# A hybrid decoder layer on one core: inverse sums turned by the matmul engine, attention outputs kept in two parts, scratch and tables moved

## The chip, the core and the metric

The kernel runs on one core of one Trainium2 chip. Its time is the device time in microseconds (us). Before the change it is 1889.12 us, the median of 3 runs (1889.0 to 1889.23). A core has five engines that run side by side, each through its own instructions in a fixed order: PE (matmul), DVE and POOL (elementwise work), ACT (activations and copies) and SP, which here only starts transfers (DMAs). ACT starts some DMAs too. An instruction that waits holds up everything behind it on its engine.

## The reference

One layer works on 16 learned meta tokens and 1024 real tokens of width 1024. Three mixers run side by side on the normalised input, their outputs go through one projection, and a gated feed-forward follows:

```python
hn = rmsnorm(h, mix_norm_g[i])
proj = hn @ w_in[i]
sb_q, sb_k, sb_v, ssm_z, ssm_xbc, ssm_dt, c_q, c_kv, k_r = jnp.split(proj, split_at, axis=-1)
o_sb  = stick_breaking_attention(sb_q, sb_k, sb_v, valid)      # 8 heads of 64
o_ssm = ssd_mixer(ssm_z, ssm_xbc, ssm_dt, ...)                 # 16 heads, chunks of 128
o_mla = mla_attention(q_mla, k_mla, v_mla, valid)              # 8 heads, rotary part of 32
h = h + jnp.concatenate([o_sb, o_ssm, o_mla], axis=-1) @ w_out[i]
fn = rmsnorm(h, ffn_norm_g[i])
h = h + (jax.nn.silu(fn @ w_gate[i]) * (fn @ w_up[i])) @ w_down[i]
return rmsnorm(h, final_norm_g)[:, BLOCK:, :]
```

The softmax of `mla_attention` divides each query's row by its sum. `ssd_mixer` needs running sums of the decay, `dt * a`, inside each chunk of 128 tokens.

## The kernel before

**Precision.** Every large product is made of three matmuls: each operand is split into an upper part, rounded to the matmul type, and a lower part, what is left. The upper part is a copy on ACT and the lower one a subtraction on POOL or DVE. `dense_fm` (L129 to L142) runs such a product over column chunks, with `dpool`'s two PSUM banks (`d_ps`) for the sums and an `evac` function that takes each sum away.

**Order of work.** The program lists its work stage by stage. When it is built, a planner gives each engine a fixed order: it goes by a simulated time, takes the earliest listed instruction that is ready, and fills gaps with later stages. Tiles of one tag share a number of slots; a new tile gets a slot once the last reader of the tile that held it is done.

The stages that matter here, by lines:

- *First projections* (from L607). `raws` (L214) are four weight buffers taken from the slots that later hold the keys of the stick-breaking heads: `raws[2]` and `raws[3]` from tag `K`, which has four slots. Pair 0 of the heads takes the two other `K` slots (`sb_project`, L575); pair 1 takes those of `raws[2]` and `raws[3]`. `k_evac` (L588) writes them.
- *`step_sizes`* (L411). After the step sizes come the decay sums `AT`; three blocks of them are turned on PE into banks of the pool `tp` (two banks, `acst`), copied by ACT to `acs`, and split by DVE into three bf16 parts in `A3` (L463 to L470). `acs` is a tile of tag `cacc`, two slots. `A3` is read first in the chunk scan (L765).
- *Stick-breaking attention* (`sb_attend`, L677). For each of 8 heads and 4 pairs of query blocks, `weighted_values` (L293) turns the weights on PE (banks `ptm`, `ptg` of `tp`), splits them, multiplies them with the values and adds two halves into `oT` (64 x 256, L343), which ACT stores to `s_osb` (L349). Projections of the next pair and the convolution units fill PE in between.
- *Chunk scan and latents* (L727 to L911). `row_tile` gives tiles of tag `lraw`, four slots. Four `scaled_unit`s make the query parts; then the tables `ct` and `sn` are loaded, multiplied on POOL by the query's norm row `cq_row` (L895), and used by the rotation (L907 to L909).
- *Softmax attention* (`mla_head`, L980). The row sums of a head land in `inv` (128 x 8). DVE inverts them (L990), and a DMA on SP writes them to `s_inv` (L991). The gate units of the SSM output (`gate_units`, L524), which load `gy`, and the output projection fill PE in between.
- *Output projection* (`out_rows`, L1016). It loads four tiles of `s_osb`, splits them (L1023, L1024), and adds its products into `hT`, loaded at L1014. Two more calls take the SSM output with its norm `grow`. `xr` has 12 slots. The first `OutGroup` (L1128) then takes the softmax heads' outputs, multiplied by the inverse sums read back from `s_inv` (L1142, L1143).

The lines on which the steps turn:

```python
            dve.reciprocal(inv, inv)                                            # L990
            sp.dma_start(s_inv[c].rearrange("(i p) -> p i", p=128), inv)        # L991
            acs = fill_tile("cacc", "acs")[:16]                                 # L457
    raws = [sbq.tile([128, 1024], F32, tag=tag, name="raw") for tag in ("KS", "KS", "K", "K")]
```

Of the kernel before, what the change touches and what calls it, by code (L numbers as in the profile page):

```python
# [59 lines left out]
def tile_hybrid_block(ctx: ExitStack, tc: tile.TileContext, a: dict):  # L60
# [15 lines left out]


    s_vsb = dram.tile([T + 1, 512], F32, name="s_vsb")
    s_osb = dram.tile([4, 128, SEQ], F32, name="s_osb")
    s_omla = dram.tile([4, 128, SEQ], F32, name="s_omla")  # L80
    s_ossm = dram.tile([8, 128, SEQ], F32, name="s_ossm")
    s_h = dram.tile([8, 128, SEQ], F32, name="s_h")
# [210 lines left out]
    def weighted_values(tp, pvp, work, j, rows, V, hh, dram_out, pm, base=None):  # L293

        pe_even, pe_odd = rows
        out = pvp.tile([128, 512], F32, tag="pv", name="pv")

        def accumulate(blk, ph, pl, c, last):
            if last:
                pe.matmul(out[:64, :256], V[:, blk, hh, 0:64], pl[:, c : c + 256], start=False, stop=False)  # L300
                pe.matmul(out[:, :256], V[:, blk, hh, :], ph[:, c : c + 256], start=False, stop=True)
            else:
                pe.matmul(out[:, :256], V[:, blk, hh, :], ph[:, c : c + 256], start=False, stop=False)  # L303
                pe.matmul(out[:64, :256], V[:, blk, hh, 0:64], pl[:, c : c + 256], start=False, stop=False)

        def split(pt, n):
            nb = 4 if work is not sbb else 2
            ph = work.tile([128, 512], F32R, tag="ph", bufs=nb, name="ph")
            pl = work.tile([128, 512], F32R, tag="pl", bufs=nb, name="pl")
            act.copy(ph[:, :n], pt[:, :n])  # L310
            dve.tensor_tensor(pl[:, :n], pt[:, :n], f32(ph[:, :n]), op=ALU.subtract)  # L311
            return ph, pl

        pt = tp.tile([128, 512], F32, tag="tp", name="ptm")
        pe.transpose(pt[:META, 0:128], pe_odd[:, 0:META], ident)
        pe.transpose(pt[:META, 128:256], pe_even[:, 0:META], ident)
        act.copy(pm[:META], pt[:META, :256])
        dve.tensor_tensor(pm[32 : 32 + META], pt[:META, :256], f32(pm[:META]), op=ALU.subtract)
        pe.matmul(out[:, :256], V[:, 0, hh, :], pm, start=True, stop=False)
        for g in range(j + 1):  # L320
            last = g == j
            pt = tp.tile([128, 512], F32, tag="tp", name="ptg")
            for e in range(2):
                k0 = META + 128 * (2 * g + e)
                pe.transpose(pt[:, e * 256 : e * 256 + 128], pe_odd[:, k0 : k0 + 128], ident)  # L325
                if not (last and e == 1):
                    pe.transpose(pt[:, e * 256 + 128 : e * 256 + 256], pe_even[:, k0 : k0 + 128], ident)  # L327
            ph, pl = split(pt, 384 if last else 512)
            if last:
                pool.memset(f32(ph[:, 384:512]), 0.0)  # L330
                pool.memset(f32(pl[:, 384:512]), 0.0)
            accumulate(2 * g + 1, ph, pl, 0, False)
            accumulate(2 * g + 2, ph, pl, 256, last)
        half = work.tile([64, 256], F32, tag="half", bufs=1, name="half")
        if base is None:
            act.copy(half, out[64:128, :256])
        else:
            for e in range(2):
                c = slice(128 * e, 128 * (e + 1))
                i = 2 * j + 1 - e  # L340
                act.activation(half[:, c], out[64:128, c], AF.Identity, bias=base[64:128, hh, i : i + 1])
        oT = work.tile([64, 256], F32, tag="oT", bufs=2, name="oT")
        dve.tensor_tensor(  # L343
            oT.rearrange("p (b t) -> p b t", b=2)[:, ::-1, :],
            out[:64, :256].rearrange("p (b t) -> p b t", b=2),
            half.rearrange("p (b t) -> p b t", b=2),
            op=ALU.add,
        )
        act.dma_start(dram_out[:, 256 * j : 256 * (j + 1)], oT)  # L349

    def split_values(V, raw, rows, dst, bs):
        act.copy(V[rows, dst, :, 0:64], raw[rows, bs])
# [58 lines left out]
    def step_sizes():  # L411
# [42 lines left out]

        pool.memset(A3, 0.0)
        for i, (t0, n) in enumerate(CH_ALL):
            acs = fill_tile("cacc", "acs")[:16]  # L457
            pt = tp.tile([128, 512], F32, tag="tp", name="acst")
            for b in range(3 * i, 3 * i + 3):
                b0, w = BLOCKS[b]  # L460
                pe.transpose(pt[:16, b0 - t0 : b0 - t0 + w], AT[:w, b, :], ident[:w, :w])
            c = slice(t0, t0 + n)
            act.copy(acs[:, :n], pt[:16, :n])  # L463
            dve.tensor_copy(A3[0:16, c], acs[:, :n])
            dve.tensor_tensor(acs[:, :n], acs[:, :n], A3[0:16, c], op=ALU.subtract)
            dve.tensor_copy(A3[32:48, c], acs[:, :n])
            a2 = fl.tile([16, 384], BF16, tag="csig", name="a2")
            dve.tensor_copy(a2[:, :n], acs[:, :n])
            dve.tensor_tensor(acs[:, :n], acs[:, :n], a2[:, :n], op=ALU.subtract)
            dve.tensor_copy(A3[64:80, c], acs[:, :n])  # L470
# [178 lines left out]
    with ctx_sb as st:  # L649
# [27 lines left out]
        def sb_attend(p, proj, values):  # L677
            Q, K, KS = proj
            for h in range(2):
                for j in range(NQ // 2):  # L680
                    rows = [sb_row(Q[h], K[h], KS[h], 2 * j + e) for e in range(2)]
                    weighted_values(tp, pvp, sbb, j, rows, values[0], h, s_osb[p, 64 * h : 64 * (h + 1)], pms[j % 2], values[1])

        values = load_value_steps(sbv, sbb, 0)
        step_sizes()
# [27 lines left out]
    with ExitStack() as st:  # L713
# [171 lines left out]
        for p in range(4):  # L885
            scaled_unit([x[:, 256 * p : 256 * (p + 1)] for x in wk], 2, ck_mov, CH_ALL, T, ck_row, s_kn[p])
        cq_mov, cq_row = latent(s_cq, 3, SEQ, gq, cq_r, real, CH_REAL, 1.0 / math.sqrt(96.0))
        for p in range(4):
            if p % 2 == 0:
                wq = load_w(a["w_uq"][p // 2], 768)  # L890
            scaled_unit([x[:, 384 * (p % 2) : 384 * (p % 2 + 1)] for x in wq], 3, cq_mov, CH_REAL, SEQ, cq_row, s_qn[p])
        ct, sn = row_tile("ct"), row_tile("sn")
        sp.dma_start(ct[:, :SEQ], a["q_cos"])
        sp.dma_start(sn[:, :SEQ], a["q_sin"])
        for t in (ct, sn):  # L895
            pool.tensor_tensor(t[:, :SEQ], t[:, :SEQ], cq_row[:, :SEQ], op=ALU.mult)
        wq = load_w(a["w_uq"][2], 768)
        w1, w2 = ([x[:, 384 * e : 384 * (e + 1)] for x in wq] for e in range(2))
        rot = [row_tile("rot") for _ in range(2)]
# [22 lines left out]
    with ExitStack() as st:  # L922
# [57 lines left out]
        def mla_head(c):  # L980
            nonlocal V
            p, h = c // 2, c % 2
            if h == 0:
                V = load_values(mr, s_v, p, ml)
            proj = mla_load(c)
            inv = mr.tile([128, NQ], F32, tag="inv", bufs=2, name="inv")
            for j in range(NQ // 2):
                rows = [mla_row(proj, i, inv[:, i : i + 1]) for i in (2 * j, 2 * j + 1)]
                weighted_values(tp, pvp, mr, j, rows, V, h, s_omla[p, 64 * h : 64 * (h + 1)], pms[j % 2])
            dve.reciprocal(inv, inv)  # L990
            sp.dma_start(s_inv[c].rearrange("(i p) -> p i", p=128), inv)  # L991

        V = None
        pms = meta_tiles(mr)
# [15 lines left out]
        def xr_tile(dt=F32):  # L1010
            return xr.tile([128, 1024], dt, tag="raw", name="raw")

        for k in range(KT):
            sp.dma_start(hT[k], a["xT"][k, :, META:])  # L1014

        def out_rows(src, k0, nk, weights):  # L1016

            H, L = [], []
            for kt in range(k0, k0 + nk):
                raw, hi, lo = xr_tile(), xr_tile(F32R), xr_tile(F32R)  # L1020
                sp.dma_start(raw, src[kt])
                if src is s_osb:
                    act.copy(hi, raw)  # L1023
                    pool.tensor_tensor(lo, raw, f32(hi), op=ALU.subtract)  # L1024
                else:
                    dve.tensor_tensor(raw, raw, grow[:, :SEQ], op=ALU.mult)
                    act.activation(hi, raw, AF.Copy, scale=gssm[:, kt : kt + 1])
                    dve.scalar_tensor_tensor(lo, raw, gssm[:, kt : kt + 1], f32(hi), ALU.mult, ALU.subtract)
                H.append(hi)
                L.append(lo)  # L1030

            def mov(kt, c0, n):
                return H[kt][:, c0 : c0 + n], L[kt][:, c0 : c0 + n]

            nf = KT // nk
            for f in range(KT):
                if f % nf == 0:
                    w = load_w(weights[f // nf])

                def evac(ps, c0, n):  # L1040
                    dve.tensor_tensor(hT[f][:, c0 : c0 + n], hT[f][:, c0 : c0 + n], ps, op=ALU.add)

                dense_fm(dpool, [x[:, 128 * nk * (f % nf) :] for x in w], nk, 128, mov, CH_REAL, evac)

        out_rows(s_osb, 0, 4, a["w_o1"][0])
        out_rows(s_ossm, 0, 4, a["w_o1"][1])
        out_rows(s_ossm, 4, 2, a["w_o2"])
    tp_st.close()
# [705 lines left out]
```

## Time and profile before

| | before |
|---|---|
| median of 3 runs | 1889.12 us |
| profiled execution | 1887.26 us, of it a span of 1885.5 us from the first to the last instruction |
| mean granted PE clock | 0.962 |
| bytes moved by DMA | 182.75 MB, 97 GB/s on average |
| HBM read, written | 129.51 MB, 51.50 MB |

The profile is one execution on the chip. Its page gives the busy time of each engine, then groups of instructions, the chain of work that ended last, and what each idle time waited for. The views quoted below have these columns: the timeline gives start, duration, engine and line, operation, what is written from what, and in brackets the idle time of the engine before it with what ended it. The chain gives start, duration and what set the time in it. The table of windows gives for each stretch its length, each engine's busy time with the number of instructions, the granted PE clock, the busy share of the DMA engines and their rate. A letter q after an engine's name marks its sequencer, which issues DMAs.

### The profile page before, as it was taken

How to read it: one execution, taken by the hardware profiler on the slowest of the kernel's cores; microseconds unless marked ns; L12 is line 12 of the kernel's file. 1: busy time of each engine (PE TensorE's matmuls, PEld its weight loads, DVE VectorE, ACT ScalarE, POOL GpSimd, SP SyncE). 2: the span in 40 equal slices, each digit the busy share in tenths (PEclk: the TensorE clock that was granted, in tenths of full speed). 3: DMA queues.
4: the chain of work that ended last, by engine and by line, in shares of the span. 5: the costliest groups of instructions: out<-in, count | busy, mean ns of one | idle time of the engine just before them, and what ended most of it. 6: DMA issues, size and time to landing. Idle time of an engine off the chain costs nothing.

```text
span 1885.5 us, 26687 instructions
## 1 busy us (share of the span) xinstructions
PE 1730.0 (92%) x9724; PEld 1501.6 (80%) x9724; DVE 1322.4 (70%) x2025; ACT 866.0 (46%) x1881; POOL 880.6 (47%) x707
## 2 busy tenths in 40 slices
PE   8889999999999889996989778889999999799997
PEld 7879989999877679985878657678888888677787
DVE  8888567776546734455565699986667766899956
ACT  7555555555566546674444234432222223433333
POOL 3443244243565465553221266653344333688782
PEclk9999999999999989997999889999999999899998
DMA  4221132122634554454332513122222224733102
GB/s 151 56 73 64 57 80 74 52 60 72 167 105 139 180 164 106 107 130 150 57 72 91 129 50 112 49 86 79 82 88 83 76 75 136 280 100 109 47 0 90
DMA packets 124615, 182.75 MB, mean 97 GB/s; under 512 B 29490, under 2 KB 86804, under 8 KB 124484
## 3 DMA queue, kind: packets, MB, share of 16 engines
q1 hardware_dynamic: 105088, 165.49, 29.3%
q10 hardware_dynamic: 19396, 15.56, 2.7%
q8 instruction: 76, 1.25, 0.3%
q14 instruction: 55, 0.45, 0.1%
HBM read 129.51 MB, written 51.50 MB: 96 GB/s over the span
## 4 chain that ended last, share of the span: by engine, by line
PE 61%; DVE 15%; DMA 7%; issue 4%; POOL 3%; ACT 3%; SPq 1%; ACTq 0%; DVEq 0%; POOLq 0%
PE b_ps L1327 7%; PE b_ps L1329 7%; PE b_ps L1328 7%; PE d_ps L137 6%; PE d_ps L139 6%; PE d_ps L138 6%; DVE raw L1070 2%; DMA gy<-s_y 2%; PE b_ps L1528 2%; PE b_ps L1530 2%; PE b_ps L1529 2%; DVE op L1067 2%; PE ptg L325 1%; DMA raw<-s_ossm 1%; PE pv L303 1%
## 5 line engine op out<-in xcount | busy, mean ns | idle before, releaser
L137 PE MATMUL d_ps<-hnh,whi 128*128 128x384 f32 (+6 forms) x744 | 248.9, 335 | 7.8 <-DVE go L535 4.0
L139 PE MATMUL d_ps<-hnl,whi 128*128 128x384 f32 (+6 forms) x744 | 246.1, 331 | 0.0
L138 PE MATMUL d_ps<-hnh,wlo 128*128 128x384 f32 (+6 forms) x744 | 245.9, 331 | 0.0
L126 POOL TENSOR_TENSOR wlo<-wraw,whi 128x1024 fp32r<-128x1024 f32 (+1 forms) x51 | 124.7, 2445 | 180.9 <-ACT whi L124 171.8
L1067 POOL TENSOR_TENSOR op<-raw,op 128x512 fp32r<-128x512 f32 x113 | 174.3, 1573 | 57.2 <-ACT op L1066 54.0
L137 PEld LDWEIGHTS d_ps<-hnh,whi 128*128 128x128 f32 (+1 forms) x744 | 140.9, 189 | 12.9 <-DVE go L535 5.5
L311 DVE TENSOR_TENSOR pl<-ptg,ph 128x512 fp32r<-128x512 f32 (+1 forms) x160 | 99.5, 629 | 64.5 <-ACT ph L310 62.8
L138 PEld LDWEIGHTS d_ps<-hnh,wlo 128*128 128x128 f32 (+1 forms) x744 | 140.7, 189 | 2.3 <-issue 0.2
L139 PEld LDWEIGHTS d_ps<-hnl,whi 128*128 128x128 f32 (+1 forms) x744 | 140.6, 189 | 2.4 <-issue 0.2
L1327 PE MATMUL b_ps<-T,wh 128*128 128x512 f32 x352 | 138.4, 394 | 0.7 <-ACT T L1066 0.7
L1066 ACT CAST op<-raw 128x512 fp32r<-128x512 f32 x149 | 84.1, 618 | 117.2 <-PE d_ps L1530 46.9
L1328 PE MATMUL b_ps<-T,wl 128*128 128x512 f32 x352 | 137.1, 390 | 0.5 <-POOL wl L1067 0.5
L1329 PE MATMUL b_ps<-T,wh 128*128 128x512 f32 x352 | 137.6, 392 | 0.0
L1067 POOL TENSOR_TENSOR wlo<-raw,whi 128x1024 fp32r<-128x1024 f32 (+1 forms) x22 | 53.0, 2410 | 150.5 <-ACT whi L1066 150.5
L670 DVE TENSOR_TENSOR_SCAN cm<-cm,zcol 128x144 f32<-128x144 f32 (+3 forms) x64 | 101.2, 1586 | 13.0 <-ACT cm L668 12.2
L310 ACT CAST ph<-ptg 128x512 fp32r<-128x512 f32 (+1 forms) x160 | 85.6, 543 | 36.7 <-PE ptg L327 28.7
L1067 POOL TENSOR_TENSOR wl<-raw,wh 128x512 fp32r<-128x512 f32 x46 | 70.6, 1545 | 62.2 <-ACT wh L1066 62.2
L1070 DVE TENSOR_TENSOR raw<-raw 128x512 f32<-128x512 f32 x58 | 70.9, 1227 | 40.4 <-DMA raw<-in_w_gate_dram 35.8
L1066 ACT CAST wh<-raw 128x512 fp32r<-128x512 f32 x88 | 53.0, 616 | 73.7 <-PE b_ps L1329 66.0
L492 POOL TENSOR_TENSOR csig<-csig,cacc 128x384 f32<-128x384 f32 (+1 forms) x36 | 47.8, 1328 | 83.0 <-ACT csig L491 50.6
L487 DVE SCALAR_TENSOR_TENSOR cacc<-d_ps,cw,cacc 128x384 f32<-128x384 f32 (+3 forms) x108 | 61.8, 573 | 33.6 <-ACT cacc L480 31.5
L1528 PE MATMUL b_ps<-op 128*128 128x512 f32 x183 | 73.7, 408 | 12.6 <-DVE hF L1073 11.3
(447 smaller groups left out, 5434.3 us busy)
## 6 DMA issues: line engine op xcount, KB each, us to landing
raw<-in_w_gate_dram SPq DMA_DIRECT2D x22, 512.0 KB
raw<-in_w_up_dram SPq DMA_DIRECT2D x22, 512.0 KB
s_hid<-gs SPq DMA_DIRECT2D x44, 256.0 KB
raw<-in_w_down_dram SPq DMA_DIRECT2D x22, 512.0 KB
raw<-s_hid SPq DMA_DIRECT2D x22, 512.0 KB
wraw<-in_w_xbc_dram SPq DMA_DIRECT2D x12, 512.0 KB
wraw<-in_w_o_dram SPq DMA_DIRECT2D x10, 512.0 KB
s_xs<-csig SPq DMA_DIRECT2D x24, 192.0 KB
```

What stands on the lines that cost most here:

```text
L126: pool.tensor_tensor(lo[:, :cols], raw[:, :cols], f32(hi[:, :cols]), op=ALU.subtract)
L137: pe.matmul(ps[:m, :n], wh, mh, start=(kt == 0), stop=False)
L138: pe.matmul(ps[:m, :n], wl, mh, start=False, stop=False)
L139: pe.matmul(ps[:m, :n], wh, ml, start=False, stop=(kt == nkt - 1))
L670: dve.tensor_tensor_scan(rev, rev, zcol.to_broadcast([128, n_all]), 1.0, ALU.mult, ALU.add)
L1066: act.copy(hi, value)
L1067: eng.tensor_tensor(lo, value, f32(hi), op=ALU.subtract)
L1070: dve.tensor_tensor(out, x, y, op=ALU.subtract)
L1327: pe.matmul(banks[j], hi[:, ks], UH[u][k], start=start and k == 0, stop=False, skip_group_check=skip)
L1328: pe.matmul(banks[j], lo[:, ks], UH[u][k], start=False, stop=False, skip_group_check=skip)
L1329: pe.matmul(banks[j], hi[:, ks], UL[u][k], start=False, stop=stop and k == 3, skip_group_check=skip)
L1528: pe.matmul(banks[o], wh[:, os], hh, start=first, stop=False, skip_group_check=not start)
```

## The change

Four edits. The inverse sums of a head are turned on PE first (128 x 8 to 8 x 128, in a `tp` bank), inverted by DVE out of the bank, and stored in rows of 128. `oT` of the stick-breaking heads is split where it is made (upper part on ACT, lower on POOL), the parts are stored in `s_osbh` by ACT and `s_osbl` by SP, and `out_rows` loads them by halves, with no split of its own and with the loads of `hT` behind them. `acs` lies in `raws[2]` and `raws[3]`. `ct` and `sn` are loaded and scaled before the four query units.

```diff
@@ weighted_values
-        act.dma_start(dram_out[:, 256 * j : 256 * (j + 1)], oT)
+        c = slice(256 * j, 256 * (j + 1))
+        if base is None:
+            act.dma_start(dram_out[:, c], oT)
+        else:
+            hi, lo = (work.tile([64, 256], F32R, tag=f"oT{x}", bufs=2, name="oTs") for x in "hl")
+            act.copy(hi, oT)
+            pool.tensor_tensor(lo, oT, f32(hi), op=ALU.subtract)
+            act.dma_start(dram_out[0][:, c], f32(hi))
+            sp.dma_start(dram_out[1][:, c], f32(lo))
@@ step_sizes
-            acs = fill_tile("cacc", "acs")[:16]
+            acs = (raws[2][:16, 0:272], raws[2][:16, 512:896], raws[3][:16, 0:384])[i]
@@ query units and rotation
         cq_mov, cq_row = latent(s_cq, 3, SEQ, gq, cq_r, real, CH_REAL, 1.0 / math.sqrt(96.0))
-        for p in range(4):
...
         ct, sn = row_tile("ct"), row_tile("sn")
...
             pool.tensor_tensor(t[:, :SEQ], t[:, :SEQ], cq_row[:, :SEQ], op=ALU.mult)
+        for p in range(4):
...
@@ mla_head
-            dve.reciprocal(inv, inv)
-            sp.dma_start(s_inv[c].rearrange("(i p) -> p i", p=128), inv)
+            pt = tp.tile([128, 512], F32, tag="tp", name="invt")
+            pe.transpose(pt[:NQ, 0:128], inv, ident)
+            rows = mr.tile([NQ, 128], F32, tag="invr", bufs=1, name="invr")
+            dve.reciprocal(rows, pt[:NQ, 0:128])
+            sp.dma_start(s_inv[c].rearrange("(i p) -> i p", p=128), rows)
@@ out_rows
-        for k in range(KT):
-            sp.dma_start(hT[k], a["xT"][k, :, META:])
...
-                raw, hi, lo = xr_tile(), xr_tile(F32R), xr_tile(F32R)
-                sp.dma_start(raw, src[kt])
-                if src is s_osb:
-                    act.copy(hi, raw)
-                    pool.tensor_tensor(lo, raw, f32(hi), op=ALU.subtract)
-                else:
+                hi, lo = xr_tile(F32R), xr_tile(F32R)
+                if src is s_ossm:
+                    raw = xr_tile()
+                    sp.dma_start(raw, src[kt])
...
+            if src is not s_ossm:
+                for c0, n in CH_REAL:
+                    for e in range(nk):
+                        for dst, part in zip((H[e], L[e]), src):
+                            sp.dma_start(f32(dst[:, c0 : c0 + n]), part[k0 + e, :, c0 : c0 + n])
+                for k in range(KT):
+                    sp.dma_start(hT[k], a["xT"][k, :, META:])
```

More of the change, by code (lines that the diff above doesn't have):

```diff
@@ L78, in tile_hybrid_block @@
     s_vsb = dram.tile([T + 1, 512], F32, name="s_vsb")
-    s_osb = dram.tile([4, 128, SEQ], F32, name="s_osb")
+    s_osbh = dram.tile([4, 128, SEQ], F32, name="s_osbh")
+    s_osbl = dram.tile([4, 128, SEQ], F32, name="s_osbl")
     s_omla = dram.tile([4, 128, SEQ], F32, name="s_omla")
@@ L681, in sb_attend @@
                     rows = [sb_row(Q[h], K[h], KS[h], 2 * j + e) for e in range(2)]
-                    weighted_values(tp, pvp, sbb, j, rows, values[0], h, s_osb[p, 64 * h : 64 * (h + 1)], pms[j % 2], values[1])
+                    weighted_values(tp, pvp, sbb, j, rows, values[0], h, [x[p, 64 * h : 64 * (h + 1)] for x in (s_osbh, s_osbl)], pms[j % 2], values[1])
         values = load_value_steps(sbv, sbb, 0)
@@ L887, in tile_hybrid_block @@
         cq_mov, cq_row = latent(s_cq, 3, SEQ, gq, cq_r, real, CH_REAL, 1.0 / math.sqrt(96.0))
-        for p in range(4):
-            if p % 2 == 0:
-                wq = load_w(a["w_uq"][p // 2], 768)
-            scaled_unit([x[:, 384 * (p % 2) : 384 * (p % 2 + 1)] for x in wq], 3, cq_mov, CH_REAL, SEQ, cq_row, s_qn[p])
         ct, sn = row_tile("ct"), row_tile("sn")
@@ L896, in tile_hybrid_block @@
             pool.tensor_tensor(t[:, :SEQ], t[:, :SEQ], cq_row[:, :SEQ], op=ALU.mult)
+        for p in range(4):
+            if p % 2 == 0:
+                wq = load_w(a["w_uq"][p // 2], 768)
+            scaled_unit([x[:, 384 * (p % 2) : 384 * (p % 2 + 1)] for x in wq], 3, cq_mov, CH_REAL, SEQ, cq_row, s_qn[p])
         wq = load_w(a["w_uq"][2], 768)
@@ L1043, in out_rows @@
                 dense_fm(dpool, [x[:, 128 * nk * (f % nf) :] for x in w], nk, 128, mov, CH_REAL, evac)
-        out_rows(s_osb, 0, 4, a["w_o1"][0])
+        out_rows((s_osbh, s_osbl), 0, 4, a["w_o1"][0])
         out_rows(s_ossm, 0, 4, a["w_o1"][1])
```

## The prediction

> **What bounds the kernel now.** I read the page first, then the windows, the idle time of PE in the timeline, and the chain through the longest of it.
>
> ```profile
> span 1885.5 us, 26687 instructions
> ...
> core 0: us, PE busy (x) PEld busy (x) DVE busy (x) ACT busy (x) POOL busy (x), PEclk, DMA share, GB/s
> 200.00:480.00 280.00, 277.90 (x1895) 264.58 (x1894) 190.97 (x269) 152.56 (x342) 102.00 (x108) 1.00 0.23 68
> 690.00:830.00 140.00, 134.52 (x912) 127.25 (x910) 63.16 (x156) 92.39 (x229) 81.49 (x86) 0.98 0.53 117
> 830.00:880.00 50.00, 31.44 (x185) 27.38 (x186) 29.28 (x65) 25.60 (x60) 22.23 (x21) 0.76 0.52 154
> ```
>
> PE bounds most of it: in the stick-breaking stage it is busy for 277.90 of 280 us, at full clock; from 830 to 880 us only for 31.44 of 50, at a granted clock of 0.76. So an edit gains only where PE stands still, and costs only where it makes PE stand still. The edits' places are visible there:
>
> ```profile
> 102.51 0.66 PE L137 MATMUL d_ps<-hnh,whi 128*128 128x384 f32 x1 [2.42 <-DVE KS L595]
> 130.08 0.47 PE L325 MATMUL ptg<-ident,cm 128*128 128x128 f32 x1 [4.99 <-ACT acs L463]
> 665.49 0.69 PE L137 MATMUL d_ps<-lhi,whi 128*128 128x384 f32 x1 [5.43 <-DVE rot L907]
> 874.44 0.79 PE L137 MATMUL d_ps<-raw,whi 128*128 128x512 f32 x1 [10.55 <-ACT grow L706]
> 976.24 0.47 PE L304 MATMUL pv<-pl,V 128*64 128x256 f32 x1 [3.85 <-DVE pl L311]
> 1075.80 0.58 PE L303 MATMUL pv<-ph,V 128*128 128x256 f32 x1 [8.63 <-ACT ph L310]
> ```
>
> The chain and the queues say what stands behind the last three:
>
> ```profile
> 727.94 0.37 SPq L991 DMA_DIRECT2D s_inv<-inv  x1
> 732.17 11.55 DMA gy<-s_y
> 856.47 0.37 SPq L991 DMA_DIRECT2D s_inv<-inv  x1
> 862.71 10.12 DMA raw<-s_osb
> 872.85 1.04 ACT L1023 CAST raw<-raw 128x1024 fp32r<-128x1024 f32 x1 [11.53 <-DMA raw<-s_osb]
> 959.87 0.37 SPq L991 DMA_DIRECT2D s_inv<-inv  x1
> 960.33 13.94 DMA raw<-s_ossm
> 1056.42 11.91 DMA s_inv<-inv
> 1074.33 1.04 ACT L124 CAST whi<-wraw 128x1024 fp32r<-128x1024 f32 x1 [12.51 <-DMA wraw<-in_w_gate_dram]
> 1076.38 0.43 PE d_ps L137
> 1081.08 0.43 PE d_ps L139
> 1082.96 2.56 DMA s_omla<-oT
> ```
>
> Three transfers issued 0.5 to 6 us behind a write of `s_inv` take 10 to 14 us, and the write itself takes 11.91 us for 4 KB, against 2.56 us for the 64 KB of a head's `s_omla`. The write puts down the 1024 sums of a head one by one. ACT and DVE wait for the transfers behind it, and PE for ACT and DVE.
>
> **The inverse sums.** Removed: eight slow writes. At the end of the softmax stage ACT waits 12.51 us for a weight queued behind the last one, and holds `ph`: PE loses 8.63 us, and then the twelve matmuls from 1076.38 to 1081.08 go at 0.43 us instead of the 0.23 of this row:
>
> ```profile
> 1020.34 0.23 PE d_ps L138
> 864.24 10.21 SPq L1014 DMA_DIRECT2D hT<-in_xT_dram  x8
> L439 DVE RECIPROCAL d<-d x1: 1053/1053/1053, 100.4 to 100.4; 128x144 f32<-128x144 f32 x1
> L990 DVE RECIPROCAL inv<-inv x8: 203/203/204, 727.3 to 1056.2; 128x8 f32<-128x8 f32 x8
> ```
>
> That is 8.6 + 12 x 0.20 = 11.0 us. At 976 us DVE waits for the late `s_ossm`: 3.5 of the 3.85 us. In the gate units (690 to 830 us) PE idles only 5.5 us in all: I take 2. Added per head: one matmul, and a reciprocal of 128 columns, which by the 1053 ns for 144 costs some 0.95 us instead of 0.20, in order on DVE, with a `tp` bank held. DVE is busy 63.16 of 140 us there, so most is covered; uncovered it is 8 x (0.75 + some 0.4 for the turn) = 9 us. I take 2. Together 11 + 3.5 + 2 - 2 = +14.5 us, bounds +2 (only the 11, less the 9) to +20 (all of 11, 3.85 and 5.5).
>
> **The parts, at the output projection.** PE's 10.55 us end with the copy of `grow`, which stands on ACT behind the split of the fourth `s_osb` tile. After the change nothing there waits for a load:
>
> ```profile
> 836.66 0.44 SPq L1021 DMA_DIRECT2D raw<-s_osb  x1
> 851.56 2.26 DVE L149 TENSOR_TENSOR rc<-rc 128x8 f32<-128x8 f32 x1
> 851.46 2.34 POOL L1024 TENSOR_TENSOR raw<-raw 128x1024 fp32r<-128x1024 f32 x1
> 945.47 1.46 SPq L1021 DMA_DIRECT2D raw<-s_ossm  x2
> ```
>
> The loads double to 4 MB. By the eight `hT` loads (4 MB issued in 10.21 us) that is some 10 us from 836.66, done before the norm's chain needs PE. What is late next is `hT`, which the first sums are added to: its slots lie on the norm's column, so its first load, at 864.24 now, comes no sooner than some 862, and lands 2 to 4 us later (2.56 for `s_omla`); I leave 4 us of the 10.55 for it. With the slow matmuls behind it (as above, some 2.4) the gain is 10.55 - 4 + 2.4 = +9, bounds 0 to +13. A removed POOL subtraction also frees DVE: L149, 8 elements a partition, takes 2.26 us while POOL's L1024 runs for 2.34, and the norm's chain hangs on it: +2. Against it: the raw tile of the second SSM operand loses its early slot (it comes now behind two parts of the first eight), so three loads and one more preparation stand at 945 us: -2, bounds 0 to -5. Together +9.
>
> The Trainium skill ("DMA: Bandwidth & Descriptors", section Measured) says that transfers should be batched to 1 MiB or more, which speaks against this edit: it halves the pieces to 256 KB. Its table gives 6.15 us for one transfer of 1 MB; an estimate from that figure is 25 us for 4 MB, and the sum would be some 10 us instead of 19.5, as in rival (c). The `hT` row above, 4 MB issued in 10.21 us, does not agree with that figure where many loads are under way; no row before has such small pieces in such number.
>
> **The parts, where they are made.** 32 times a copy on ACT, a subtraction on POOL and a DMA issue on SP are added; the nearest rows give 0.37 us for the copy and 0.73 for the subtraction, and the `s_inv` rows 0.37 for an issue:
>
> ```profile
> L336 ACT COPY half<-pv x32: 369/371/372, 702.9 to 1082.1; 64x256 f32<-64x256 f32 x32
> L533 POOL TENSOR_TENSOR gy<-gy,gs x24: 725/1006/1022, 678.4 to 840.5; 128x384 f32<-128x384 f32 x16, 128x256 f32<-128x256 f32 x8
> ```
>
> That is 12 us of ACT, 23 of POOL and 12 of SP, in a stage where ACT is busy 152.56 and POOL 102.00 of 280 us. ACT already waited for `oT` to issue its store; now `ph` and the sigmoids queue behind one more copy. PE's cover is the convolution work, and it leaves 2.1 us idle in 280. I take -2; with that cover gone it is 32 x 0.37 on ACT's path, -12.
>
> **The rotation.** `ct` and `sn` come 25 us sooner. They need the norm row, whose second half is written at 635, and POOL is then free:
>
> ```profile
> 635.11 0.60 ACT L706 ACTIVATE lrow<-d_ps 128x512 f32<-128x512 f32 x1 [0.92 <-PE d_ps L181]
> 644.91 1.82 POOL L126 TENSOR_TENSOR wlo<-wraw,whi 128x768 fp32r<-128x768 f32 x1 [7.89 <-ACT whi L124]
> 656.43 0.33 SPq L860 DMA_DIRECT2D s_qn<-nope  x1
> ```
>
> POOL's 7.89 us hold both products (2 x 2.34, the time of L1024, of the same shape). But the tables now keep two of four `lraw` slots, so the second `rot` tile waits for the store issued at 656.43, some 3 us, and the tables' loads stand ahead of a weight on SP. Of the 5.43 us I take +4, bounds -2 (both products in the way of POOL's weight split once) to +5.4.
>
> **The decay sums.** The 4.99 us fall away, for the third `acs` has its own space. But that space is a `K` slot of the next pair, whose first evacuation came long before the split:
>
> ```profile
> 97.32 0.36 ACT L592 CAST K<-d_ps 64x272 fp32r<-64x272 f32 x1
> 120.02 0.82 PE L461 MATMUL acst<-ident,AT 16*16 16x16 f32 x6
> 123.83 0.27 PE L315 MATMUL ptm<-ident,cm 128*16 128x128 f32 x1
> L470 DVE CAST A<-acs x3: 292/352/352, 129.2 to 136.6; 16x384 bf16<-16x384 f32 x2, 16x272 bf16<-16x272 f32 x1
> ```
>
> Now the keys wait for the split's end. Two chunks fill the two banks of `d_ps` by 100 us, and PE has no third bank, nor attention, which starts only behind `acst`. Freed of the keys' evacuations, ACT and DVE reach `acst` near 110; three chains of six DVE steps of some 0.4 us take 7.4. The third chunk comes at about 119 instead of 102.51: 16.5 us of PE, of which attention, starting 13 us sooner, fills some 5. Against it the 4.99 fall away: -6, bounds -14 to +5.
>
> **Sum.** 14.5 + 9 - 2 + 4 - 6 = 19.5 us. Against the profiled execution's 1887.26 this is 1867.8; that execution stands 1.86 under the median, so for the median I predict 1869.6, rounded 1870.
>
> **The rivals.**
> (a) *The keys don't wait.* The planner holds their chunks back and fills with other work: the decay edit gains its 5 us, 11 more than above: 1859. For it: PE has convolution work; against it: that needs the same two banks. 0.17.
> (b) *Slower: the stick-breaking stage pays for the split.* The store of the lower part sits on SP, in order, behind POOL, and the weights of the fillers behind it; ACT's copy delays `ph`. At 1.1 us of PE for each of 32 tiles (0.37 + 0.73 in a row) that is 35 us instead of 2: 1870 + 33 = 1903. It decides from (19.5 + 2)/32 = 0.67 us a tile. For it: PE has no idle time left there; against: ACT and POOL are half idle. 0.14.
> (c) *Small pieces.* If each 256 KB load costs what 512 KB cost (1.28 us by the `hT` row), sixteen take 20.5 us, `hT` comes 10 us later, and the output projection gains nothing: 1879. 0.14.
> (d) *Not the scattered write.* If the transfers near it are late for other reasons (DMA share 0.52 there), the 14.5 shrink to -2, and the rest nets 5 - 2: 1886, about no change. 0.08.
> My forecast has 0.47.
>
> **How the numbers follow.** No change is within 0.2%, 3.8 us, about what a measurement of this kernel can tell. Faster: the forecast, (a) and (c), 0.78; same: most of (d), 0.07; slower: (b) and a little of (d), 0.15. The range goes from the sum with the decay and projection at their upper bounds (19.5 + 11 + 4, and the inverse sums' 5.5: 40, 1849) to the edge of (d), 1887; above lies (b), and little below.
>
> **What would show it.** Right: `s_inv` lands within 3 us, no 10 us gap near 870 and 1070, and the transfers behind it take 2 to 5 us; a PE gap of 8 us or more between 99 and 120, ended by a `K` or `KS` copy, for the decay step; the rotation's gap under 2 us; the stage from 200 to 480 still 99% busy. Wrong: idle PE of over 20 us in the stick-breaking stage, or 10 us transfers that stay without the scattered writes.

## The result, and the profile after

| | before | after |
|---|---|---|
| median, first chip | 1889.06 us (1885.44 to 1889.23, 4 runs) | 1854.86 us (1853.53 to 1856.16, 4 runs) |
| ratio, first chip | | 0.9827 (0.9812 to 0.9842) |
| median, second chip | 1878.6 us (9 runs) | 1855.99 us (4 runs) |
| ratio, second chip | | 0.9874 (0.9856 to 0.9892) |
| profiled execution, first chip | 1887.26 us | 1856.16 us |

The change gains 34.2 us where the prediction said 19.5, and on a second chip 22.6: the changed kernel takes the same time on both, the kernel before does not.

First, the windows of both kernels, cut at the same work: the last matmul of the chunk scan, of the rotation, of the gate units, of the softmax stage and its output projection, and the first operand product of the feed-forward. Columns are the length, then the busy time of each engine, the granted clock and the DMA share. Before:

```profile
core 0: us, PE busy (x) PEld busy (x) DVE busy (x) ACT busy (x) POOL busy (x), PEclk, DMA share, GB/s
0.00:656.40 656.40, 616.24 (x4224) 564.69 (x4226) 465.48 (x758) 378.31 (x902) 277.59 (x261) 0.98 0.31 94
656.40:672.40 16.00, 10.52 (x58) 9.82 (x55) 6.70 (x15) 0.36 (x1) 7.00 (x3) 0.89 0.37 128
672.40:836.40 164.00, 156.78 (x1049) 148.73 (x1048) 70.27 (x175) 106.12 (x257) 95.39 (x102) 0.98 0.54 126
836.40:1083.20 246.80, 210.20 (x1150) 177.77 (x1149) 150.02 (x289) 105.82 (x250) 69.59 (x67) 0.91 0.39 104
1083.20:1202.30 119.10, 94.21 (x385) 75.22 (x384) 113.01 (x146) 51.08 (x89) 76.39 (x47) 0.90 0.21 74
1202.30:1885.50 683.20, 642.01 (x2869) 525.34 (x2867) 516.93 (x646) 224.30 (x384) 354.61 (x227) 0.97 0.28 94
```

After:

```profile
0.00:668.00 668.00, 625.27 (x4226) 570.56 (x4226) 469.17 (x758) 390.30 (x934) 310.23 (x295) 0.96 0.32 96
668.00:676.90 8.90, 8.85 (x58) 8.28 (x53) 6.67 (x14) 0.29 (x1) 2.41 (x1) 1.00 0.57 177
676.90:836.70 159.80, 154.56 (x1048) 147.65 (x1047) 72.95 (x177) 105.68 (x256) 96.80 (x103) 0.99 0.46 130
836.70:1047.70 211.00, 201.70 (x1159) 170.80 (x1157) 143.49 (x287) 99.46 (x244) 56.90 (x61) 0.98 0.38 121
1047.70:1171.00 123.30, 96.83 (x387) 77.70 (x386) 113.42 (x146) 52.65 (x91) 79.05 (x48) 0.85 0.25 88
1171.00:1854.30 683.30, 640.70 (x2869) 524.61 (x2867) 519.44 (x647) 223.99 (x384) 355.93 (x227) 0.98 0.28 94
```

Read row against row, the spans' 31.2 us come apart: 11.6 lost up to the end of the scan, 7.1 gained in the rotation, 4.2 in the gate units, 35.8 in the softmax stage with the projection, 4.2 of that given back right behind it, and nothing after. In the fourth row PE's idle time (length less busy) falls from 36.6 to 9.3 us, and the same matmuls take 8.5 us less, at a clock of 0.98 instead of 0.91. In the first row it is the other way round: 2.6 us more idle time, and 9.0 us more for the same matmuls.

The rows of the changed kernel that answer to the places the prediction named. First two windows, then waits of PE and ACT in the timeline (in brackets the idle time and what ended it), then the transfers on the chain of waits between 700 and 1100 us:

```profile
200.00:480.00 280.00, 279.34 (x1924) 267.05 (x1923) 196.37 (x272) 158.82 (x363) 118.53 (x131) 1.00 0.25 74
830.00:880.00 50.00, 45.20 (x288) 39.72 (x287) 35.78 (x85) 30.60 (x77) 17.74 (x23) 0.97 0.71 240
```

```profile
107.96 0.85 PE L461 MATMUL acum<-d,tri 128*128 128x144 f32 x2 [6.34 <-DVE d L459]
124.06 0.38 ACT L601 CAST K<-d_ps 64x272 fp32r<-64x272 f32 x1 [2.60 <-DVE A L479]
677.69 0.42 PE L138 MATMUL d_ps<-hnh,whi 128*128 128x384 f32 x1 [0.36 <-DVE rot L916]
1062.19 0.79 PE L1196 MATMUL b_ps<-op 128*128 128x512 f32 x1 [8.85 <-ACT op L1081]
1075.06 0.79 PE L1196 MATMUL b_ps<-op 128*128 128x512 f32 x1 [5.11 <-ACT op L1081]
```

```profile
927.69 3.73 DMA raw<-s_ossm
1048.27 6.82 DMA raw<-s_omla
```

The stick-breaking stage is still full. The gaps of 10.55 us near 870 and 8.63 near 1070 are gone, and on the chain two transfers are left where before there were eleven. The keys of pair 1 wait for the third part of the split (`A`, L479) until 124.06 us. At the first products of the softmax heads' output stand two gaps now, 8.85 and 5.11 us, where the kernel before has one of 5.00 and a second of 2.12:

```profile
1093.87 0.80 PE L1181 MATMUL b_ps<-op 128*128 128x512 f32 x1 [5.00 <-ACT op L1066]
```

### The profile page after: what moved, and what is told of

Same layout as the page of the kernel before. It is cut to its first block, busy times and chain, and to the rows that moved or that the text cites. A ratio compares the mean times of both kernels' runs of the same rounds, so it can differ in the third digit from the quotient of the medians.

```text
span 1854.3 us, 26858 instructions
## 1 busy us (share of the span) xinstructions
PE 1727.9 (93%) x9732; PEld 1499.6 (81%) x9732; DVE 1325.1 (71%) x2025; ACT 872.4 (47%) x1909; POOL 901.3 (49%) x735
## 4 chain that ended last, share of the span: by engine, by line
PE 69%; DVE 18%; issue 4%; DMA 3%; ACT 3%; POOL 2%; SPq 0%; DVEq 0%; ACTq 0%; POOLq 0%
PE d_ps L138 7%; PE d_ps L139 7%; PE d_ps L140 7%; PE b_ps L1342 7%; PE b_ps L1344 7%; PE b_ps L1343 7%; DVE raw L1085 2%; DVE op L1082 2%; PE b_ps L1543 2%; PE ptg L326 2%; PE b_ps L1545 2%; PE b_ps L1544 2%; PE pv L305 1%; PE pv L304 1%; PE ptg L328 1%
## 5 line engine op out<-in xcount | busy, mean ns | idle before, releaser
L679 DVE TENSOR_TENSOR_SCAN cm<-cm,zcol 128x144 f32<-128x144 f32 (+3 forms) x64 | 106.3, 1669 | 12.7 <-ACT cm L677 12.0
L1085 DVE TENSOR_TENSOR raw<-raw 128x512 f32<-128x512 f32 x58 | 76.6, 1325 | 38.2 <-DMA raw<-in_w_gate_dram 34.2
L1543 PE MATMUL b_ps<-op 128*128 128x512 f32 x183 | 73.5, 406 | 12.9 <-DVE hF L1088 11.6
L1088 DVE TENSOR_TENSOR hF<-hF,b_ps 128x512 f32<-128x512 f32 (+1 forms) x96 | 59.0, 635 | 36.1 <-PE b_ps L1609 18.2
```

Of the source, the lines that this page charges most:

```text
L679: dve.tensor_tensor_scan(rev, rev, zcol.to_broadcast([128, n_all]), 1.0, ALU.mult, ALU.add)
L1085: dve.tensor_tensor(out, x, y, op=ALU.subtract)
L1543: pe.matmul(banks[o], wh[:, os], hh, start=first, stop=False, skip_group_check=not start)
```

## What a stage takes in each kernel that ran

All experiments are read with this table. Each number comes from one trace: the time between the last matmul of the scan (`yd`), of the rotation (`d_ps<-lhi,whi`), of the gate units (`d_ps<-hnh,whi`) and the first of the feed-forward (`b_ps<-T,wh`). The experiments ran on three further chips: the single edits on one; the change again, and with an edit left out or altered, on the second chip of the result; the last three kernels and the kernel before on another. So rows of different chips stand side by side here, while each ratio is taken on one chip. Behind the last column every trace has another 680 to 687 us, which does not follow the edits.

| kernel | to the scan's end | rotation | gate units | softmax end, projection | time against before |
|---|---|---|---|---|---|
| before, first chip | 656.4 | 15.9 | 163.8 | 366.2 | |
| before, another chip | 655.2 | 16.4 | 158.6 | 359.3 | |
| inverse sums only | 656.9 | 16.3 | 157.0 | 340.7 | 0.9900 (0.9887 to 0.9912) |
| parts only | 658.5 | 16.7 | 153.2 | 362.7 | 0.9983 (0.9971 to 0.9995) |
| decay sums only | 676.5 | 21.6 | 157.6 | 357.1 | 1.0109 (1.0094 to 1.0123) |
| tables only | 656.1 | 8.9 | 159.3 | 358.6 | 0.9940 (0.9929 to 0.9952) |
| change without decay | 658.0 | 8.9 | 159.0 | 331.9 | 0.9838 (0.9824 to 0.9851) |
| change, third decay chunk apart | 656.4 | 8.9 | 159.7 | 334.9 | 0.9826 (0.9812 to 0.9839) |
| change without inverse | 666.7 | 8.9 | 159.3 | 345.3 | 0.9930 (0.9917 to 0.9943) |
| change again | 667.9 | 8.9 | 159.2 | 332.4 | 0.9874 (0.9856 to 0.9892) |
| all but parts (third chunk apart) | 655.7 | 8.9 | 159.1 | 339.1 | 0.9855 (0.9838 to 0.9872) |
| write in 32-byte pieces only | 655.1 | 15.8 | 157.3 | 328.6 | 0.9826 (0.9809 to 0.9842) |
| third chunk apart, whole rows | 657.0 | 8.9 | 159.1 | 332.1 | 0.9828 (0.9811 to 0.9844) |

## The experiments

**Each edit alone**, on the kernel before. The diffs are those of the change, one at a time: the `invt` turn at `mla_head`; the parts in `weighted_values` and `out_rows`; the line of `acs`; the move of `ct` and `sn`.

```diff
-            sp.dma_start(s_inv[c].rearrange("(i p) -> p i", p=128), inv)
+            pe.transpose(pt[:NQ, 0:128], inv, ident)
+            dve.reciprocal(rows, pt[:NQ, 0:128])
+            sp.dma_start(s_inv[c].rearrange("(i p) -> i p", p=128), rows)
```

> The kernel before with only the inverse sums turned on TensorE and written by rows. The prediction gave this edit +14.5 us (1874.6), and left the 10.55 us of idle TensorE at 874 us to the parts. Theory S: the write of 1024 sums one by one holds up every transfer issued within some 10 us of it, the load of s_osb at 862.71 us too; then this edit alone also removes most of that gap, and the time is 1889 - 14.5 - 8 = 1866 or less, with the idle time of TensorE from 836 to 1083 us (36.6 us) under 16. Theory P: the gap at 874 us is the split's own; then the gap stays at 8 us or more, and the time is near 1875. Rival (d), not the write: no transfer behind it gets shorter, and the time is 1889 or above.

Measured: 1859.41 us against 1877.65, a gain of 18.8 by the ratio, which lies between the two theories (22.5 or more, and 14.5). The traces decide. Each fence has the long waits of PE near 860 and 1065 us in the timeline: the first of the kernel before on another chip, the second of the inverse edit alone, the third of the parts alone, with the wait of DVE that stands behind the first of them.

```profile
866.86 0.79 PE L137 MATMUL d_ps<-raw,whi 128*128 128x512 f32 x1 [9.12 <-ACT grow L706]
1063.65 0.58 PE L303 MATMUL pv<-ph,V 128*128 128x256 f32 x1 [6.45 <-ACT ph L310]
```

```profile
848.59 0.47 PE L304 MATMUL pv<-pl,V 128*64 128x256 f32 x1 [5.22 <-DVE pl L311]
1063.30 0.80 PE L1184 MATMUL b_ps<-op 128*128 128x512 f32 x1 [9.86 <-ACT op L1069]
```

```profile
868.03 0.69 DVE L1053 TENSOR_TENSOR hT<-hT,d_ps 128x512 f32<-128x512 f32 x1 [9.37 <-DMA hT<-in_xT_dram]
868.77 0.79 PE L138 MATMUL d_ps<-raw,whi 128*128 128x512 f32 x1 [5.28 <-DVE hT L1053]
1067.78 0.58 PE L304 MATMUL pv<-ph,V 128*128 128x256 f32 x1 [7.40 <-ACT ph L311]
```

With the write by rows alone, the gap ahead of the first projection (9.12 us) is gone, although the loads of `s_osb` and the split stand as before; what is left near it is a wait of the attention, 5.22 us, earlier, and behind the softmax stage the 6.45 us have become 9.86 at the next products. With the parts alone it is still there, 5.28 us, now ended by `hT`, whose load is issued 3.6 us behind the slow write and waits in place of `s_osb`. So in both kernels the gap hangs on the write, as theory S says; the load that is caught behind it differs.

> The kernel before with only the stick-breaking outputs stored as upper and lower parts. The prediction gave it +9 at the projection and -2 where the parts are made: 1882. Theory S: the loads of the parts lie ahead of the slow write at 856 us or behind it, and hT now lies behind it; what is won from the split is partly lost to hT, and the time is 1883 to 1887. Theory P: the gap is the split's, TensorE idles under 4 us between 860 and 880 us, and the time is 1880 or less. Rival (b) would show here as a stick-breaking stage longer by 20 us or more: 1900.

Measured: 1874.04 us against 1877.65, 3.2 us by the ratio. Rival (b) needed a stick-breaking stage 20 us longer; the scan ends 3.3 us later than in the kernel before.

> The kernel before with only the place of the decay sums changed. The prediction gave it -6 us (1895), bounds -14 to +5; rival (a), keys that don't wait, +5 (1884). The two traces show keys that wait until 124 us, TensorE idle 3.9 us more up to 656 us, and 8.5 us more of busy time for the same matmuls, at a granted clock of 0.89 instead of 0.97 from 75 to 200 us. If both losses come from this edit, the time is 1889 + 12 = 1901; if the slower matmuls come from the parts' additional work instead, 1893.

Measured: 1899.4 us against 1877.65, a loss of 20.5, more than expected. The keys wait as in the changed kernel, and there are long gaps in the scan (6.31 us) and the rotation (8.76 in place of 5.22 to 5.43):

```profile
123.98 0.38 ACT L592 CAST K<-d_ps 64x272 fp32r<-64x272 f32 x1 [3.12 <-DVE A L470]
...
646.14 2.07 PE L797 MATMUL yo<-bc,S 128*128 128x128 f32 x8 [6.31 <-DVE y L807]
690.97 0.69 PE L137 MATMUL d_ps<-lhi,whi 128*128 128x384 f32 x1 [8.76 <-DVE rot L907]
```

The chain of waits through the first of the two holds a store that takes 9.51 us, where such a store on the chain takes 3.36 us in the kernel before on another chip and 4.49 in the changed kernel on the second:

```profile
631.57 9.51 DMA s_y<-y
```

So part of the loss lies in how the transfers at the scan's end fall together in this order of work; that the waiting keys bring this about was not shown.

Where all four edits are made, the tables take the rotation's gap away, and the first two columns of the table lose 5.2 us against the kernel before on another chip (676.8 against 671.6), not 26.5.

> The kernel before with only the rotation tables scaled sooner. The prediction gave it +4 (1885); the two traces show the rotation stage 7.1 us shorter, 5.43 of it idle time and 1.7 slower matmuls behind it, so 1882. If the products take POOL's time from the weight splits instead, 1889 or above.

Measured: 1867.58 us against 1877.65, 11.3 by the ratio. The rotation takes 8.9 us instead of 16.4, which is 7.5; the rest of the ratio has no place in the two traces, whose other columns agree within 1 us. The trace of the kernel before is of an execution 7 us below the median of its chip.

**The change less one edit, and the change again**, on one chip.

> The changed kernel with the decay sums put back in their two old buffers. The prediction's -6 us says 1849; the decay edit alone cost 1899.4 against 1877.65, 1.1%, and if that holds in the changed kernel too, this is 20 us faster than the changed kernel beside it, 1835. If the loss beside the decay edit was the parts' work in the stick-breaking stage, it is within 4 us of the changed kernel.

```diff
-            acs = (raws[2][:16, 0:272], raws[2][:16, 512:896], raws[3][:16, 0:384])[i]
+            acs = fill_tile("cacc", "acs")[:16]
```

Measured: 1849.02 us, 7.0 faster than the changed kernel beside it; the scan ends 9.9 us sooner. So the decay edit costs in the whole change too, though a third of what it costs alone.

> The changed kernel with the third decay chunk in a buffer of its own that no key needs (the spare one of the convolutions' raw tiles), the first two in their old buffers. The theory of the waiting keys says that both are had: the 4.99 us of idle TensorE at 125 us stay away and the keys don't wait, so it is 4 to 5 us faster than the change without the decay edit. If the old wait for a buffer cost nothing that lasts, it equals that one within 2 us.

```diff
-            acs = (raws[2][:16, 0:272], raws[2][:16, 512:896], raws[3][:16, 0:384])[i]
+            acs = fill_tile("craw" if i == 2 else "cacc", "acs")[:16]
```

Measured: 1846.13 us, 9.9 faster than the changed kernel; its lead of 2.9 over the kernel above lies within both intervals. The old wait hardly shrinks. PE's wait for `acs` in the change without the decay edit, then with the third chunk apart:

```profile
128.70 0.47 PE L326 MATMUL ptg<-ident,cm 128*128 128x128 f32 x1 [4.60 <-ACT acs L472]
```

```profile
127.35 0.33 PE L326 MATMUL ptg<-ident,cm 128*128 128x128 f32 x1 [3.51 <-ACT acs L472]
```

So the missing buffer was about 1 us of it. The rest is ACT's order: its third copy to `acs` (126.83) stands behind a copy of a query that waits for DVE, and DVE is busy with the split of the first two chunks:

```profile
126.22 0.58 ACT L610 CAST Q<-d_ps 64x512 fp32r<-64x512 f32 x1 [3.81 <-DVE Q L611]
```

The prediction took all of it to vanish with the buffer.

> The changed kernel with the sums inverted and written one by one, as before. The inverse edit alone gained 18.8 us on the kernel before. If its gain is its own, this is 18 to 19 us slower than the changed kernel; if it overlaps with the parts at the projection (both remove one 10 us gap), 8 to 12; if the two need each other (parts alone gained 3.2 us only), 25 or more.

Measured: 1865.48 us, 9.5 slower than the changed kernel: in the whole change the turn is worth half of its 18.8 alone, as the overlap at the projection said. This kernel has the slow write and no gap ahead of the first projection: the load of `hT`, issued 7.65 us behind the write of 852.60, takes 6.21 us (10.30 in the kernel with the parts alone, 3.6 us behind), and PE waits 1.12 us for it.

```profile
860.25 6.21 DMA hT<-in_xT_dram
867.32 0.50 PE L138 MATMUL d_ps<-raw,whi 128*128 128x512 f32 x1 [1.12 <-DVE hT L1053]
```

So the slow write alone does not make the gap: it takes a needed load close behind it.

> The changed kernel once more, beside the three others on one chip: between 0.981 and 0.985 of the kernel before if the gain doesn't depend on the chip; nearer to 0.99 if the chip on which the single edits ran, where the kernel before was 11 us faster, has less to gain.

Measured: 0.9874, less than on the first chip, because the kernel before is 10.5 us faster here.

**The kernel before on another chip, all but the parts, the write by itself, the size of the pieces.**

> The kernel before once more, for its trace on this chip. On two chips it took 1877.65 and 1878.6 us, on the first 1889.06, while the changed kernel took 1855 to 1856 on two. If the scattered write's price is what differs between chips, its landing times and the three idle times of TensorE behind it (3.84, 8.63 and 10.55 us on the first) are shorter here by some 10 us together, and the stretch up to 656 us is the same within 2 us. If the whole program is faster here, the stretches without such a write are shorter too.

Measured: 1871.32 us in one run (the others beside it 1873.5 to 1881.24). Its stage up to the scan's end differs from the first chip's by 1.2 us; gate units and projection are 5.2 and 6.9 shorter. The transfers near the writes, from the chain of waits, are shorter by 0.5 to 2.3 us each than the first chip's 10.12, 13.94 and 11.91:

```profile
855.66 9.58 DMA raw<-s_osb
951.34 12.71 DMA raw<-s_ossm
1046.38 9.59 DMA s_inv<-inv
```

Of the 15.9 us between the two traces 12.1 lie in these two columns, the stages with the slow write, which the change removes. But PE's three idle times behind it (10.55, 8.63 and 3.85 us on the first chip; 9.12, 6.45 and 2.90 here) are only 4.6 us shorter together, not 10, and this execution stands 7 us below the median of its chip. Why the chips differ stays open.

> The kernel before with the inverse sums turned, the tables scaled sooner and the third decay chunk in the spare raw tile, but no parts: what the parts are worth when the slow write is gone. Theory S (the gap at 874 us was the write's, and the parts find nothing left there): within 3 us of the change with that decay buffer, 1846.1, or faster. Theory P (the split held the projection up by itself, +9 by the prediction): 1853 or more.

Measured: 1849.93 us, 0.9855. Against the same kernel with the parts (0.9826, on the second chip) the parts are worth some 5 us; in the traces 4.2 are gained in the last column (339.1 to 334.9) and 0.7 lost up to the scan's end. Against the last kernel below, which has the parts in whole rows and ran on this same chip (1844.15), it is 5.8, with 7.0 in the last column. Between the two theories, then: not 0, and not 9.

> The kernel before, whose inverse sums are written in one piece of 32 bytes for each partition, 128 pieces in place of 1024 of 4 bytes, without a turn on TensorE; the order of the sums in memory is then another than their reader takes. It separates the write from the turn. If the number of pieces sets the price, the transfers behind the write take 2 to 6 us and the time is that of the inverse edit alone (0.990 of the kernel before), or 1 to 4 us less if the turn costs anything. If any write below 512 bytes stalls the queues alike, nothing is gained: 0.998 or above.

```diff
-            sp.dma_start(s_inv[c].rearrange("(i p) -> p i", p=128), inv)
+            sp.dma_start(s_inv[c].rearrange("(p i) -> p i", i=8), inv)
```

The reader is left as it was and takes the sums in another order than they are written, so this kernel is of use for its time alone. Measured: 1845.52 us against 1878.3, a gain of 32.7 from one line, 13.9 more than the turned sums where at most 4 were expected, and more than the whole change gains on the second chip. Two things are in it. The packets (the page's line on DMA) fall by 7169, which is 8 writes of 1024 pieces made into 128 (7168):

```profile
DMA packets 117446, 182.74 MB, mean 99 GB/s; under 512 B 22322, under 2 KB 79636, under 8 KB 117316
```

(before: 124615 packets, 29490 of them under 512 B). With that, the long transfers go, as with the turn. The other thing is the order of PE's work. Here the last head's last matmul (`pv`) runs at 1033.92 us, and 36 of the projection's 480 matmuls stand behind it:

```profile
1033.92 0.28 PE L301 MATMUL pv<-ph,V 128*128 128x256 f32 x1
...
1046.13 0.39 PE L139 MATMUL d_ps<-raw,whi 128*128 128x512 f32 x1
```

They cover the store, the load and the scaling of that head's output. With the turn, PE's order puts the last head behind all of the projection; the inverse edit alone:

```profile
1046.47 0.39 PE L139 MATMUL d_ps<-raw,whi 128*128 128x512 f32 x1
1046.70 0.28 PE L303 MATMUL pv<-ph,V 128*128 128x256 f32 x1
...
1048.46 0.28 PE L301 MATMUL pv<-ph,V 128*128 128x256 f32 x1
```

and 9.86 us of idle time follow; in the kernel with 32-byte pieces the longest wait there is

```profile
1053.09 1.62 PE L1183 MATMUL b_ps<-op 128*128 128x512 f32 x3 [2.80 <-DVE op L1067]
```

Of the 18.9 us between the two traces, 12.1 lie in the last column, 340.7 against 328.6 (by the ratios the two ways are 13.9 us apart, 0.0074 of 1878). Whether the turn's own instructions or the order that the planner made around them is to blame was not separated.

> The changed kernel with the third decay chunk in the spare raw tile, and the parts loaded in eight pieces of 512 KB instead of sixteen of 256 KB. Rival (c), dear small pieces, says that the halves cost up to 10 us; then this is faster than 1846.1 by 3 us or more. If pieces of both sizes cost by their bytes, it is the same within 2 us, or slower, since the first half of the columns then comes later.

```diff
-                for c0, n in CH_REAL:
-                    for e in range(nk):
-                        for dst, part in zip((H[e], L[e]), src):
-                            sp.dma_start(f32(dst[:, c0 : c0 + n]), part[k0 + e, :, c0 : c0 + n])
+                for e in range(nk):
+                    for dst, part in zip((H[e], L[e]), src):
+                        sp.dma_start(f32(dst), part[k0 + e])
```

Measured: 1844.15 us, 0.9828 against 0.9826: the same. Rival (c) falls: between 256 and 512 KB these runs show no difference. The rule of 1 MiB and more (the Trainium skill, "DMA: Bandwidth & Descriptors", section Measured) is not settled by this, for both sizes lie below it.

Of the kernels that keep the order of the sums, the fastest are the change with the third decay chunk apart (1846.13 us beside 1855.99 for the changed kernel) and the same with whole rows (1844.15, on another chip). A write in 32-byte pieces whose reader takes the sums in that order, together with the other edits, was not run.

## Why the prediction was right, and where it was off

The direction and the range held, and the main reason was right: the transfers near the slow writes were long because of those writes. The size was 14.7 us short. Of the profiled execution, predicted 1867.8 and measured 1856.16, the difference of 11.6 us comes from three places: 3.6 less up to the scan's end (11.6 lost, not 8), 3.1 more in the rotation, 12.2 more from the gate units on (35.7 net, not 23.5). The other 3.1 us are how the two profiled executions stand to their medians. On the second chip the gain of 22.6 lies near the 19.5, but by luck: set against the kernel before on another chip, 12.7 us are lost up to the scan's end (not 8), 7.5 gained in the rotation (not 4), 0.6 lost in the gate units (not 2 gained) and 26.9 gained behind them (not 21.5), so the errors cancel.

- **Inverse sums, +14.5: too small.** Alone they gained 18.8 where the kernel before is 11.4 us faster than on the first chip. Removing the slow write without a turn gained 32.7, beyond the upper bound of 20. The step that failed is the one that gave PE's 10.55 us at 874 to the split of `s_osb`: the row said `ACT grow`, ACT stood behind `raw<-s_osb`, and that load stood behind the write of 856.47 us. Without the write alone the gap of 9.12 us is gone; without the split alone 5.28 are left. The turn's 2 us are the other mis-sized term: up to 14, unless the order is to blame. In the gate units the prediction took 2 us; 4.2 came on the first chip, and 1.6 with this edit alone (158.6 to 157.0).
- **Parts at the projection, +9: too large by itself.** 4 to 7 us where the slow write is gone, and about nothing alone. With the other edits but the turn the gap is gone although the write is there, and the last column has 345.3 us, against 357.1 to 359.3 in the kernels without parts and turn; no run has tables and decay sums without the parts, so how much of this is theirs stays open. `hT` being late next was right, and its price too (5.28 against 4), but only close behind the slow write.
- **What is late next, not seen.** The 8.85 us and 5.11 us that end at 1062.19 and 1075.06, 7 us more than the 5.00 and 2.12 before. Without the 8.63 us of waiting at `ph`, PE is through sooner, and the load of the last head's `s_omla` (6.82 us on the chain) and its scaling are late. The kernel with the 32-byte pieces, where projection work stands behind the last head, has no such gap.
- **Parts where made, -2: right.** The scan ends 0.7 to 3.3 us later with them (656.4 against 655.7 beside the other edits, 658.5 against 655.2 alone).
- **Tables, +4: too small.** 7.1 us: all 5.43 of the gap (the next wait for a `rot` tile, at 677.69, is 0.36), and 1.7 of slow matmuls behind it (10.52 busy to 8.85), which the prediction counted at the projection but not here. The wait for the second `rot` tile and the blocked weight split did not show.
- **Decay sums, -6: right in kind, too small.** 7.0 by the medians, 9.9 by the traces, and 20.5 alone, below the bound of -14 (there the late store at the scan's end is part of it). The keys waited as described (124.06, ended by `A`), PE's gap was 6.34 us instead of 8 or more, and it stands ahead of `acum`, ended by DVE's `d` and not by a copy of a key. Most of the price in the changed kernel is not idle time: the attention that starts early runs in small pieces between waits for DVE, near half clock. The windows of the changed kernel, then of the kernel before:

```profile
110.00:120.00 10.00, 7.11 (x28) 4.43 (x27) 9.43 (x16) 6.31 (x14) 3.90 (x5) 0.61 0.21 63
120.00:130.00 10.00, 6.23 (x29) 5.04 (x28) 9.71 (x16) 6.99 (x17) 5.04 (x4) 0.56 0.01 2
130.00:140.00 10.00, 9.88 (x57) 8.86 (x55) 8.09 (x12) 6.03 (x13) 3.53 (x4) 0.93 0.11 26
```

```profile
110.00:120.00 10.00, 9.94 (x44) 7.65 (x42) 6.40 (x9) 3.74 (x8) 6.35 (x6) 1.00 0.46 130
120.00:130.00 10.00, 5.09 (x39) 4.52 (x38) 8.77 (x12) 4.23 (x8) 4.96 (x3) 0.97 0.19 53
```

The prediction counted what attention would fill, at full speed. The Trainium skill ("TensorE: Matmul & The Clock Gate", Part 1) says that an idle stretch of some 3.4 us halves the clock until PE has been busy as long again; the trace agrees, with the clock down behind the 6.34 us and up again once PE is busy for 9.88 of 10 us.

Rival (a) falls with the row of 124.06, (b) with 279.34 of 280 us busy, (c) with the whole rows, (d) with the inverse edit alone.

## What to carry to other kernels

Follow a long wait through the queue to the transfer ahead of the late one: a gap that names ACT or a split may belong to a small write issued 6 us before. Price idle time together with the slow matmuls behind it, and ask of each removed wait what it had been hiding. When a planner lays out the order, edits do not add up (alone they gain 12.8 us in sum, together 22.6), so try the change less each edit, not only each edit alone.

## What the runs showed of the hardware

A write of 4 KB in 1024 pieces of 4 bytes took 11.91 us, and transfers issued up to 6 us behind it took 10 to 14. The same bytes in 128 pieces of 32 landed in 2.6 us (the median of eight), and no transfer on the chain behind them took over 7.93. Whether the number or the size of the pieces is dear was not separated. The Trainium skill ("DMA: Bandwidth & Descriptors", Specifications) puts the bound for full rate at 512 bytes; both forms lie below it, and only one hurts here. The last such write took 9.17 to 12.27 us in the six traces that have it, and 9.17, 10.89 and 12.27 on one chip, so these figures show no difference between chips. The load of `hT` took 10.30 us when issued 3.6 us behind the write and 6.21 at 7.65 us; these are two kernels, and the distance alone was not varied.
